# Seven products on three PSUM banks: order and evictions of a Strassen-Winograd pair in an encoder layer

## The chip, the core and the metric

The kernel runs on one core of a Trainium2 chip. The metric is the device time of one execution in microseconds (us); lower is better.

## The reference

One layer of a streaming-encoder trunk on 256 tokens of width 2048, in float32: a SwiGLU feed-forward, a hybrid mixer (chunked mLSTM and stick-breaking attention in parallel branches, merged by gates), a second SwiGLU feed-forward, each with a layer norm behind it, and a gated per-layer embedding at the end.

```python
def _swiglu(x, w1, w3, w2):
    return (jax.nn.silu(x @ w1) * (x @ w3)) @ w2

def reference(x, p, ...):
    x = _layer_norm(ALPHA * x + 0.5 * _swiglu(x, ffn1_w1, ffn1_w3, ffn1_w2), ln1_g, ln1_b)
    mix = _hybrid_mixer(x, w_in, ...)      # x @ w_in: 11 column groups, two branches, two gates
    x = _layer_norm(ALPHA * x + mix, ln2_g, ln2_b)
    x = _layer_norm(ALPHA * x + 0.5 * _swiglu(x, ffn2_w1, ffn2_w3, ffn2_w2), ln3_g, ln3_b)
    x = x + jax.nn.sigmoid(x @ w_ple_gate) * (p @ w_ple_proj)
```

w1 and w3 are 2048 x 5632, w2 is 5632 x 2048.

## The kernel before

**Precision.** Every large matmul is made of three: weights and activations are each split into a rounded high part and the rest, and high x high, high x low and low x high are summed in PSUM. A *weight tile* holds 256 rows by 512 columns, 128 x 2 x 512. `split_one` makes its two parts: ScalarE copies the high part (line 1264), VectorE subtracts for the low one (line 1268). A *unit* is six matmuls (lines 1319 to 1321, twice): one weight tile against 128 tokens.

**Plain groups.** `group` multiplies a block of 512 columns in the plain way: each weight tile serves two units, one for each half of the tokens.

**Pairs.** Of the rest, two blocks of 512 columns are taken together and multiplied by seven products in place of eight (Strassen in Winograd's form). The 2 x 2 blocks are the two halves of the tokens and two halves of the rows on one side, two row halves and two column blocks on the other. `seven` writes the list of units for such a pair: products 1 to 7, each over four *quads* (four steps of 512 rows along the 2048), 28 units, and each of their weight tiles serves a single unit. In the feed-forwards a pair is 512 columns of w1 beside 512 of w3 (`up7`, nine pairs in each of the two), in the mixer two blocks of w_in (`both7`, five pairs). `act` holds the transposed activations, `act.forms` their sums (made by `form_turn`).

**Sums of weights.** Products 5, 6 and 4 use one tile, b11, on which b12, b22 and b21 are added one after the other; product 7 adds b22 onto b12. An addition is either a VectorE instruction (`plus`, line 366) or a DMA issued by GpSimd that adds from HBM (`plus_load`, line 372): in quads of `loaded` products 5 and 7 use the DMA, and all else VectorE. `Weight.loads` lists the raw tiles that must be loaded for a tile, `frees` those that are done with after its split, and `soon` the sums that are issued right behind its split. The sum of product 5 is in `soon` of product 1 of its quad, since it overwrites b11.

**Order and limits.** `seven` returns the units as: product 1 of the first quad; then, quad by quad, product 1 of the next quad and 5, 7, 6, 3; then 4 and 2 of all quads in turn. `in_line` sets one pair behind the other, with the next one's first unit four units before the end. `weave` spreads the pairs' units evenly among the plain groups' (in a feed-forward 252 among 172). Everything is issued in one program order: after each unit, `splits_due` splits weights as long as no more than the second number of `HELD` are in flight, and `loads` issues loads as long as no more raw tiles than the first number are held.

```python
HELD = {"ffn": (11, 6), "mix": (6, 6), "woven": (9, 6), "wide": (11, 6)}
```

A raw tile marked `early` (b12 of a DMA sum) is loaded three places ahead of its turn (`AHEAD`). Work that follows a product is set into the order by `Sched` with delays from `DELAY`.

**PSUM.** Each product has a bank of its own, but 2, which goes on top of 1. As a product ends, `done` is called. In `up7` product 1 is copied out by ScalarE (line 598), 2 goes through Silu on ScalarE, and VectorE adds 6, 7, 5, 4 and 3 to the copies straight from their banks (lines 592 and 630); `both7` is alike (lines 420, 426, 436, 439).

Of the kernel before, what the change touches and what calls it, by code (L numbers as in the profile page):

```python
# [16 lines left out]
D = 2048  # L17
# [6 lines left out]
COL = 512  # L24
# [12 lines left out]

HEAD = 20
# [17 lines left out]
    "alpha": 24.0, "away": 5.0, "sig": 5.0, "form": 18.0, "ln_turn": 3.6, "ln_step": 2.1, "gb": 14.0, "h": 8.0, "silu": 6.0, "late": 9.0, "last": 5.0, "rest": 1.2, "mt": 3.2,  # L56
# [132 lines left out]
def kernel(  # L189
# [159 lines left out]
    def seven(wa, ca, wb, cb, rows, cols, act, done, loaded):  # L349
# [7 lines left out]
        accs = {m: {} for m in range(1, 8)}  # L357
        accs[2] = accs[1]

        def unit(m, i, tile, src, half, sub):  # L360
            return Unit(tile, half, accs[m], src, i, sub, i == 0 and m != 2, i == n - 1,
                        lambda ps, t, m=m: done(m, ps))
# [12 lines left out]
        one, rest, then = [], [], []  # L375
        for i in range(n):
            b11, b12, b22, b21 = (rows_of(w, (4 * i + sub) * P, c, cols)
                                  for w, c, sub in ((wa, ca, 0), (wb, cb, 0), (wb, cb, 2), (wa, ca, 2)))
            m1 = Weight(b11, [b11], [])
            if i in loaded[0]:  # L380
                m5 = Weight(b11, [], [], plus_load(b11, b12.src[0]), m1)
                m5.by_load = True
                m1.soon.append(m5)
            else:
                m5 = Weight(b11, [b12], [], plus(b11, b11, b12), m1)
            if i in loaded[1]:
                assert i in loaded[0]
                m7 = Weight(b12, [b12], [b12], plus_load(b12, b22.src[0]), m1)
                m7.by_load = b12.early = True
                (m6 if i else m1).soon.append(m7)  # L390
            else:
                m7 = Weight(b12, [b12, b22] if i in loaded[0] else [b22], [b12], plus(b12, b12, b22),
                            m1 if i in loaded[0] else m5)
            m6 = Weight(b11, [b22] if i in loaded[1] else [], [], plus(b11, b11, b22), m5)
            m2 = Weight(b21, [], [b21])
            m4 = Weight(b11, [b21], [b11], plus(b11, b11, b21), m6)
            one.append(unit(1, i, m1, act, 0, 0))
            rest.append([unit(5, i, m5, act.forms, 0, 0), unit(7, i, m7, act.forms, 1, 0),
                         unit(6, i, m6, act.forms, 0, 2), unit(3, i, Weight(b22, [], [b22]), act.forms, 1, 2)])
            then += [unit(4, i, m4, act, 1, 2), unit(2, i, m2, act, 0, 2)]  # L400
            then[-1].onto = True
        first = []
        for i in range(n):
            first += one[i + 1:i + 2] + rest[i]
        return one[:1], first, then
# [9 lines left out]
    def both7(w, ca, cb, act, dest, ready, loaded):  # L415

        r, held = {}, {}

        def put(k, t, a, b, op):
            nc.vector.tensor_tensor(out=r[k, t], in0=a, in1=b, op=op)  # L420

        def rest():
            u = r[0, 1]
            put(0, 1, held[7], u, ALU.add)
            z = r[1, 1] = dest(1, 1)
            nc.vector.scalar_tensor_tensor(out=z, in0=u, scalar=-1.0, in1=held[5],
                                           op0=ALU.mult, op1=ALU.subtract)
            ready(1, 1)
# [3 lines left out]
        def done(m, ps):  # L432
            held[m] = ps
            if m == 1:
                r[0, 1] = dest(0, 1)
                nc.scalar.copy(r[0, 1], ps)
            elif m == 2:
                r[0, 0] = dest(0, 0)
                nc.scalar.copy(r[0, 0], ps)
                ready(0, 0)  # L440
            elif m == 6:
                r[1, 0] = dest(1, 0)
                put(0, 1, ps, r[0, 1], ALU.add)
                put(1, 0, held[5], r[0, 1], ALU.add)
                sched.spawn(rest(), DELAY["rest"])
            elif m == 4:
                sched.until(lambda: (1, 1) in r)
                put(0, 1, ps, r[0, 1], ALU.add)
                ready(0, 1)
            elif m == 3:  # L450
                put(1, 0, ps, r[1, 0], ALU.subtract)
                ready(1, 0)
# [112 lines left out]
    def ffn(w1, w3, w2, act, norm, skew=True, ahead=()):  # L565
# [22 lines left out]
        def up7(c):  # L588
            r, held = {}, {}
# [3 lines left out]

            def done(m, ps):
                held[m] = ps
                if m == 1:
                    r["u"] = temp()
                    nc.scalar.copy(r["u"][:], ps)
                elif m == 2:
                    r["g0"] = temp()  # L600
                    activate(r["g0"][:], ps, ACT.Silu)
                    sched.spawn(late(r["u"], r["v"], r["z"], r["g0"]), DELAY["late" if c < n - 1 else "last"])
                elif m == 6:
                    u, v, z = r["u"], temp(), temp()
                    both(u[:], ps, u[:], ALU.add)
                    both(v[:], held[5], u[:], ALU.add)
                    r["v"], r["z"] = v, z
                    sched.spawn(rest(), DELAY["rest"])
                elif m == 4:
                    sched.until(lambda: "rest" in r)  # L610
                    both(r["u"][:], ps, r["u"][:], ALU.add)
                    sched.spawn(silu(r["u"]), DELAY["silu"])
                elif m == 3:
                    both(r["v"][:], ps, r["v"][:], ALU.subtract)

            def rest():
                both(r["u"][:], held[7], r["u"][:], ALU.add)
                both(r["z"][:], held[5], r["u"][:], ALU.add)
# [4 lines left out]
            def silu(x):  # L623
                activate(x[:], x[:], ACT.Silu)
                return
                yield

            def late(u, v, z, g0):
                both(v[:], v[:], g0[:], ALU.mult)
                nc.vector.scalar_tensor_tensor(out=z[:], in0=z[:], scalar=-1.0, in1=u[:], op0=ALU.mult, op1=ALU.mult)  # L630
                drop(2)
                sched.spaced(turn(v, c, 0), DELAY["h"], TURN_GAP)
                sched.spaced(turn(z, c, 1), DELAY["h"] + 2.0, TURN_GAP)
# [3 lines left out]
            return seven(w1, c * COL, w3, c * COL, D, COL, act, done, (range(c == 1, 4), range(c == 1, 4)))  # L637
# [452 lines left out]
    every = (range(4), range(4))  # L1090
# [8 lines left out]
    later = (range(1, 4), range(1, 4))  # L1099
# [114 lines left out]
    splits = {}  # L1214
# [40 lines left out]
    def split_one():  # L1255
# [14 lines left out]
        for f in w.soon:  # L1270
            assert f.raw.tile is not None
            f.make()
            f.made = True
# [83 lines left out]
```

## Time and profile before

| | |
|---|---|
| median of 3 runs | 2169.44 us (2167.12 to 2170.17) |
| the profiled execution: its time | 2169.55 us |
| its span, first to last instruction | 2167.7 us |
| granted TensorE clock | 1.000 |
| TensorE (PE) busy | 2157.4 us |
| VectorE (DVE) busy | 1893.7 us |
| ScalarE (ACT) busy | 1347.1 us |
| GpSimd (POOL) busy | 218.2 us |
| moved by DMA | 535.98 MB |

The page of a profile gives, for one execution, busy times of the engines, a chart in 40 slices, the chain of work that ended last, and groups of instructions: line, engine, operation, tiles and shapes, count, then busy us and mean ns of one, then the idle time just before them and what ended it. "L1264" is line 1264 of the kernel. `raw` are weight tiles as loaded, `split` their parts, `mm` the PSUM banks of units, `ms` those of transposes and other small matmuls, `temp` and `big` tiles in SBUF.

### The profile page before, as it was taken

The page shows a single profiled execution, that of the slowest core. Times are in us where ns is not written, and L with a number is a line of the kernel's source. Part 1 is how long each engine was busy: PE and PEld are TensorE (multiplying, and loading weights), DVE is VectorE, ACT ScalarE, POOL GpSimd, SP SyncE. Part 2 cuts the span into 40 slices and gives each one's busy share as a digit, 9 for nine tenths or more (in the row PEclk, how much of TensorE's full clock was granted, in tenths as well). Part 3 has the DMA queues.
Part 4 walks back from the last instruction along what each step waited for, and adds up shares of the span by engine and source line. Part 5 has one row for each costly group of instructions (what it writes and reads, how often), then busy time and mean ns, then how long its engine had stood idle before and what let it go on. Part 6 is the DMA issues. An engine that isn't in the chain of part 4 may idle for free.

```text
span 2167.7 us, 27662 instructions
## 1 busy us (share of the span) xinstructions
PE 2157.4 (100%) x9798; PEld 1783.9 (82%) x9798; DVE 1893.7 (87%) x2088; ACT 1347.1 (62%) x1658; POOL 218.2 (10%) x186
## 2 busy tenths in 40 slices
PE   9999999999999999999999999999999999999999
PEld 7888888888888888888888888888888888888887
DVE  6899999999998898887878975799999999999974
ACT  7656666656655765677866554556556656656572
POOL 0111111111100000101010000011111111111000
PEclk9999999999999999999999999999999999999999
DMA  9899899999994667978898976679989999999642
GB/s 349 215 275 270 249 270 275 272 280 268 266 318 140 215 218 219 242 218 203 260 272 260 273 260 203 201 192 279 267 245 276 279 266 277 257 276 294 237 166 87
DMA packets 283179, 535.98 MB, mean 247 GB/s; under 512 B 17144, under 2 KB 34464, under 8 KB 283040
## 3 DMA queue, kind: packets, MB, share of 16 engines
q1 hardware_dynamic: 234624, 440.87, 59.9%
q0 software_dynamic: 48416, 93.33, 23.9%
q8 instruction: 77, 1.26, 0.2%
q14 instruction: 62, 0.51, 0.1%
HBM read 527.85 MB, written 6.29 MB: 246 GB/s over the span
## 4 chain that ended last, share of the span: by engine, by line
PE 93%; issue 2%; DMA 2%; DVE 2%; ACT 0%; POOL 0%; SPq 0%; POOLq 0%; DVEq 0%; ACTq 0%
PE mm L1319 30%; PE mm L1321 30%; PE mm L1320 30%; DMA raw<-in_ffn_w_dram 2%; PE ms L293 1%; DVE split L1268 1%; PE ms L519 0%; DVE raw L366 0%; PE ms L984 0%; PE ms L906 0%; PE ms L921 0%; PE ms L997 0%; POOL raw L372 0%; PE ms L1008 0%; DMA actT<-ymaway 0%
## 5 line engine op out<-in xcount | busy, mean ns | idle before, releaser
L1264 ACT CAST split<-raw 128x1024 fp32r<-128x1024 f32 (+1 forms) x1089 | 1089.4, 1044 | 513.8 <-DMA raw<-in_ffn_w_dram 172.7
L1268 DVE TENSOR_TENSOR split<-raw,split 128x1024 fp32r<-128x1024 f32 (+1 forms) x1089 | 1277.8, 1212 | 141.5 <-ACT split L1264 134.6
L1319 PE MATMUL mm<-split,actT 128*128 128x512 f32 x3064 | 1203.0, 393 | 1.2 <-DVE big L420 1.2
L1321 PE MATMUL mm<-split,actT 128*128 128x512 f32 x3064 | 1189.5, 388 | 0.6 <-DVE actT L300 0.6
L1320 PE MATMUL mm<-split,actT 128*128 128x512 f32 x3064 | 1188.4, 388 | 1.0 <-DVE split L1268 1.0
L1321 PEld LDWEIGHTS mm<-split,actT 128*128 128x128 f32 x3064 | 575.8, 188 | 120.7 <-DVE actT L300 1.4
L1320 PEld LDWEIGHTS mm<-split,actT 128*128 128x128 f32 x3064 | 576.6, 188 | 115.9 <-DVE split L1268 3.4
L1319 PEld LDWEIGHTS mm<-split,actT 128*128 128x128 f32 x3064 | 576.3, 188 | 115.5 <-issue 2.6
L372 POOL DMA_DIRECT2D raw<-in_ffn_w_dram x140 | 169.7, 1441 | 1204.9 <-DVE split L1268 809.6
L366 DVE TENSOR_TENSOR raw<-raw 128x1024 f32<-128x1024 f32 x190 | 231.6, 1220 | 1.6
L372 POOL DMA_DIRECT2D raw<-in_w_in_dram x38 | 46.0, 1426 | 505.7 <-DVE split L1268 432.5
L295 ACT CAST actT<-ms 128x512 fp32r<-128x512 f32 x60 | 35.1, 586 | 77.7 <-PE ms L293 73.2
L644 DVE SCALAR_TENSOR_TENSOR big<-mm,big 128x512 f32<-128x512 f32 x112 | 76.5, 685 | 2.9 <-PE mm L1321 2.8
L592 DVE TENSOR_TENSOR temp<-mm,temp 128x512 f32<-128x512 f32 x108 | 73.1, 686 | 1.8 <-PE mm L1321 0.6
L300 DVE TENSOR_TENSOR actT<-ms,actT 128x512 fp32r<-128x512 f32 x60 | 41.1, 687 | 16.5 <-ACT big L299 11.0
L243 ACT ACTIVATE temp<-mm 128x512 f32<-128x512 f32 (+1 forms) x36 | 20.3, 570 | 49.5 <-PE mm L1321 49.5
L239 ACT ACT_TABLE_LOAD x34 | 43.6, 1283 | 0.6
L288 DVE TENSOR_TENSOR actT<-temp,actT 128x512 fp32r<-128x512 f32 x40 | 26.5, 689 | 17.3 <-ACT actT L287 17.2
L1180 DVE TENSOR_TENSOR temp<-temp,big 128x512 f32<-128x512 f32 (+1 forms) x10 | 5.8, 583 | 26.4 <-ACT temp L243 26.4
L287 ACT CAST actT<-temp 128x512 fp32r<-128x512 f32 x40 | 23.9, 620 | 8.0 <-DVE temp L311 7.4
L243 ACT ACTIVATE rstd<-mv,eps 128x1 f32<-128x1 f32 x6 | 1.8, 295 | 41.8 <-DVE mv L502 41.8
L1123 DVE SCALAR_TENSOR_TENSOR big<-big,mm 128x512 f32<-128x512 f32 x8 | 5.5, 686 | 25.3 <-PE mm L1321 25.3
(133 smaller groups left out, 605.6 us busy)
## 6 DMA issues: line engine op xcount, KB each, us to landing
raw<-in_ffn_w_dram SPq DMA_DIRECT2D x527, 512.0 KB, 6.9
raw<-in_w_in_dram SPq DMA_DIRECT2D x144, 512.0 KB, 5.3
raw<-in_ffn_w_dram POOLq DMA_DIRECT2D x140, 512.0 KB, 9.8
raw<-in_w_in_dram POOLq DMA_DIRECT2D x38, 512.0 KB, 9.0
raw<-in_w_out_dram SPq DMA_DIRECT2D x32, 512.0 KB, 5.5
raw<-in_w_ple_gate_dram SPq DMA_DIRECT2D x32, 512.0 KB, 5.2
raw<-in_w_in_dram SPq DMA_DIRECT2D x56, 256.0 KB, 3.8
raw<-in_w_up_m_dram SPq DMA_DIRECT2D x16, 512.0 KB, 6.8
```

What stands on the lines that cost most here:

```text
L239: nc.scalar.preload_act_table_set(table[0])
L295: nc.scalar.copy(dst[:, 0], ps[:])
L300: nc.vector.tensor_tensor(out=dst[:, 1], in0=ps[:], in1=dst[:, 0], op=ALU.subtract)
L366: nc.vector.tensor_tensor(out=out.tile[:, :, :cols], in0=a.tile[:, :, :cols], in1=b.tile[:, :, :cols], op=ALU.add)
L372: nc.gpsimd.dma_start(out=out.tile[:, :, :cols], in_=src, accum_op=ALU.add)
L592: nc.vector.tensor_tensor(out=out, in0=a, in1=b, op=op)
L644: nc.vector.scalar_tensor_tensor(out=xs, in0=ps, scalar=0.5, in1=xs, op0=ALU.mult, op1=ALU.add)
L1264: nc.scalar.copy(hi[:, ks], r[:, ks])
L1268: nc.vector.tensor_tensor(out=lo[:, ks], in0=r[:, ks], in1=hi[:, ks], op=ALU.subtract)
L1319: nc.tensor.matmul(ps, hi, w[0][:, k, :u.cols], start=first, stop=False, skip_group_check=u.onto)
L1320: nc.tensor.matmul(ps, hi, w[1][:, k, :u.cols], start=False, stop=False, skip_group_check=u.onto)
L1321: nc.tensor.matmul(ps, lo, w[0][:, k, :u.cols], start=False, stop=last, skip_group_check=u.onto)
```

## The change

The order of a pair's units is written out (`CHAIN`), and products 1, 6, 7 and 4 accumulate one after the other on one bank, without a new start; ScalarE copies the bank as it stands after each of 1, 6 and 7. Products 5 and 3 do the same on a second bank, and 2 has a third. So the partial sums that VectorE had made are made by the accumulation; signs are turned where the running sums ask for it, one of them in `form_turn`. Quads no longer alternate product by product: product 1 of all quads comes first, with 5 close behind, then 6, 3 and 2, then 7, and 4 at the end. VectorE makes the sum for product 4 right behind the split of product 2 of that quad; the DMA for product 7 is issued behind the splits named in `CHAIN_BEHIND`. Sums asked for whose tile is not loaded yet wait in `asked`. The work after the products is spread: product 2's Silu, then one half of the outputs after product 3 (delay `late0`) and the other after product 4.

```diff
+CHAIN = [(1, 0), (1, 1), (1, 2), (5, 0), (1, 3), (5, 1), (5, 2), (5, 3), (6, 0), (6, 1), (3, 0), (2, 0), (6, 2), (3, 1),
+         (2, 1), (6, 3), (3, 2), (2, 2), (7, 0), (2, 3), (7, 1), (7, 2), (7, 3), (3, 3), (4, 0), (4, 1), (4, 2), (4, 3)]
+CHAIN_BEHIND = (2, 1), (6, 3), (3, 2), (2, 2)
...
-        nc.vector.tensor_tensor(out=s34[:, r], in0=a[0][:, r], in1=s12[:, r], op=ALU.add)
+        nc.vector.scalar_tensor_tensor(out=s34[:, r], in0=a[0][:, r], scalar=-1.0, in1=s12[:, r],
+                                       op0=ALU.mult, op1=ALU.subtract)
...
-        accs = {m: {} for m in range(1, 8)}
-        accs[2] = accs[1]
+        accs = {m: {} for m in (1, 2, 5)}
+        accs[6] = accs[7] = accs[4] = accs[1]
+        accs[3] = accs[5]
...
+            u = Unit(tile, half, accs[m], src, i, sub, i == 0 and m in (1, 2, 5), i == n - 1,
+                     lambda ps, t, m=m: done(m, ps))
...
+        def with_split(w, after):
+            w.by_load = True
+            after.soon.append(w)
...
+            m1 = W[1, i] = Weight(b11, [b11], [])
+            if i in loaded:
                 m5 = Weight(b11, [], [], plus_load(b11, b12.src[0]), m1)
+                with_split(m5, m1)
+                m7 = Weight(b12, [b12], [b12], plus_load(b12, b22.src[0]), m1)
+                b12.early = True
...
+            W[6, i] = Weight(b11, [b22], [], plus(b11, b11, b22), m5)
+            W[3, i] = Weight(b22, [], [b22])
+            W[2, i] = Weight(b21, [b21], [b21])
+            W[4, i] = Weight(b11, [], [b11], plus(b11, b11, b21), W[6, i])
+            with_split(W[4, i], W[2, i])
+        behind = CHAIN_BEHIND
         for i in range(n):
-            first += one[i + 1:i + 2] + rest[i]
-        return one[:1], first, then
+            with_split(W[7, i], W[behind[i]] if i in loaded else W[3, i])
...
+        units = [unit(m, i, W[m, i], *at[m]) for m, i in CHAIN]
+        return units[:1], units[1:], []
...
             def done(m, ps):
                 if m == 1:
+                    keep("g", ps)
+                elif m == 5:
+                    keep("z", ps)
+                elif m == 6:
+                    keep("v", ps)
                 elif m == 2:
+                    both(r["g"][:], ps, r["g"][:], ALU.add)
+                    sched.spawn(silu(r["g"]), DELAY["silu"])
+                elif m == 3:
+                    both(r["v"][:], ps, r["v"][:], ALU.add)
+                    sched.spawn(late(0, r["v"], r["g"]), DELAY["late0"])
+                elif m == 7:
+                    keep("u", ps)
                     sched.spawn(rest(), DELAY["rest"])
                 elif m == 4:
                     sched.until(lambda: "rest" in r)
+                    activate(r["u"][:], ps, ACT.Silu)
+                    sched.spawn(late(1, r["z"], r["u"]), DELAY["late" if c < n - 1 else "last"])
 
             def rest():
+                both(r["z"][:], r["u"][:], r["z"][:], ALU.add)
...
+        asked.extend(w.soon)
+        for f in asked[:]:
+            if f.raw.tile is not None:
+                f.make()
+                f.made = True
+                asked.remove(f)
```

`keep` is a ScalarE copy of the bank into a tile; `both7` changes in the same way, with copies of 1, 5, 6, 7 and 4 and three VectorE operations.

More of the change, by code (lines that the diff above doesn't have):

```diff
@@ L55 @@
 DELAY = {
[L56 removed]
+    "alpha": 24.0, "away": 5.0, "sig": 5.0, "form": 18.0, "ln_turn": 3.6, "ln_step": 2.1, "gb": 14.0, "h": 8.0, "silu": 6.0, "late": 9.0, "late0": 1.0, "last": 5.0, "rest": 1.2, "mt": 3.2,
     "sbt": 4.6, "g0": 3.0, "g1": 4.0, "g2": 12.0, "cv0": 1.0, "cv1": 5.0, "cv2": 1.3,
@@ L356, in seven @@
         n = rows // (4 * P)
-        accs = {m: {} for m in range(1, 8)}
-        accs[2] = accs[1]
+        accs = {m: {} for m in (1, 2, 5)}
+        accs[6] = accs[7] = accs[4] = accs[1]
+        accs[3] = accs[5]
         def unit(m, i, tile, src, half, sub):
-            return Unit(tile, half, accs[m], src, i, sub, i == 0 and m != 2, i == n - 1,
-                        lambda ps, t, m=m: done(m, ps))
+            u = Unit(tile, half, accs[m], src, i, sub, i == 0 and m in (1, 2, 5), i == n - 1,
+                     lambda ps, t, m=m: done(m, ps))
+            u.onto = m not in (1, 2, 5)
+            return u
         def plus(out, a, b):
@@ L373, in plus_load @@
             return make
-        one, rest, then = [], [], []
+        def with_split(w, after):
+            w.by_load = True
+            after.soon.append(w)
+        W = {}
         for i in range(n):
@@ L394, in seven @@
[L394 to L400, printed above, removed]
@@ L415, in both7, with keep, less @@
     def both7(w, ca, cb, act, dest, ready, loaded):
-        r, held = {}, {}
-        def put(k, t, a, b, op):
-            nc.vector.tensor_tensor(out=r[k, t], in0=a, in1=b, op=op)
-        def rest():
[L423 to L428, printed above, removed]
+        r = {}
+        def keep(k, t, ps):
+            if (k, t) not in r:
+                r[k, t] = dest(k, t)
+            nc.scalar.copy(r[k, t], ps)
+        def less(k, t, a):
+            nc.vector.scalar_tensor_tensor(out=r[k, t], in0=a, scalar=-1.0, in1=r[k, t], op0=ALU.mult, op1=ALU.subtract)
+            ready(k, t)
+        def rest():
+            less(1, 1, r[0, 1])
             return
@@ L1088, in ups @@
         return parts[0] + parts[1]
-    every = (range(4), range(4))
+    every = range(4)
     def gate_dest(g):
@@ L1097, in gate_dest @@
         return dest
-    later = (range(1, 4), range(1, 4))
+    later = range(1, 4)
     def pair(g):
```

87 lines of the change are left out of this document (28 added, 59 removed).

## The prediction

> **What bounds the kernel now.** I read the page first, from its busy shares to its chain, then the matmuls in order of time, then busy times by stretch, then the waits. Sections 1, 2 and 4 of the page:
>
> ```profile
> PE 2157.4 (100%) x9798; PEld 1783.9 (82%) x9798; DVE 1893.7 (87%) x2088; ACT 1347.1 (62%) x1658; POOL 218.2 (10%) x186
> PE   9999999999999999999999999999999999999999
> DVE  6899999999998898887878975799999999999974
> PEclk9999999999999999999999999999999999999999
> ...
> PE 93%; issue 2%; DMA 2%; DVE 2%; ACT 0%; POOL 0%; SPq 0%; POOLq 0%; DVEq 0%; ACTq 0%
> ```
>
> TensorE is busy in every slice at the full granted clock, and the chain that ended last is 93% TensorE. A busy matmul is not yet one at its peak, so I look at the distance from start to start. Timeline of PE, the first and last of 24 rows, and the group of one of the three matmul lines:
>
> ```profile
> 399.68 0.39 PE L1320 MATMUL mm<-split,actT 128*128 128x512 f32 x1
> ...
> 404.89 0.39 PE L1319 MATMUL mm<-split,actT 128*128 128x512 f32 x1
> ...
> L1319 PE MATMUL mm<-split,actT 128*128 128x512 f32 x3064 | 1203.0, 393 | 1.2 <-DVE big L420 1.2
> ```
>
> 23 distances in 5.21 us are 0.2265 us each, and 3 x 3064 = 9192 of these matmuls need 2082 us. What is left of the span, 86 us, goes to the 606 small matmuls and to gaps. Span less busy time is 2167.7 - 2157.4 = 10.3 us.
>
> Where is that idle time, and how near are the suppliers? Busy time by stretch (start, tail, first feed-forward, second, mixer):
>
> ```profile
> 0.00:60.00 60.00, 57.41 (x254) 46.73 (x255) 42.18 (x56) 41.50 (x58) 3.55 (x9) 1.00 0.91 320
> ...
> 2050.00:2168.00 118.00, 112.65 (x513) 92.98 (x511) 74.09 (x98) 56.87 (x92) 0.00 (x0) 1.00 0.36 125
> ...
> 150.00:600.00 450.00, 450.00 (x2016) 372.80 (x2015) 425.01 (x419) 279.92 (x297) 67.78 (x56) 1.00 0.95 270
> 1540.00:1950.00 410.00, 409.98 (x1834) 338.98 (x1833) 385.86 (x379) 249.66 (x265) 61.30 (x51) 1.00 0.95 268
> 660.00:1150.00 490.00, 489.64 (x2325) 406.17 (x2325) 404.68 (x541) 338.20 (x507) 36.35 (x30) 1.00 0.76 219
> ```
>
> The columns are PE, PEld, DVE, ACT, POOL, clock, DMA share, GB/s. Start and tail hold 2.6 + 5.0 us of the idle time (the last stretch reaches 0.3 us past the span); 2.7 us lie between them, and that is all that a change which leaves the matmuls as they are can plainly win. In the feed-forwards VectorE is at 94% and the DMA engines at 0.95. TensorE never waits, yet both are close behind it. The mixer has room: 83% and 0.76.
>
> **The change, part by part.** *Matmuls.* Each pair has 28 units of six matmuls before and after; fewer banks and start flags take none away. Cost 0.
>
> *Evictions.* The split of a weight tile, and the rows of what goes and what comes:
>
> ```profile
> L1264 ACT CAST split<-raw 128x1024 fp32r<-128x1024 f32 (+1 forms) x1089 | 1089.4, 1044 | 513.8 <-DMA raw<-in_ffn_w_dram 172.7
> L1268 DVE TENSOR_TENSOR split<-raw,split 128x1024 fp32r<-128x1024 f32 (+1 forms) x1089 | 1277.8, 1212 | 141.5 <-ACT split L1264 134.6
> L366 DVE TENSOR_TENSOR raw<-raw 128x1024 f32<-128x1024 f32 x190 | 231.6, 1220 | 1.6
> L592 DVE TENSOR_TENSOR temp<-mm,temp 128x512 f32<-128x512 f32 x108 | 73.1, 686 | 1.8 <-PE mm L1321 0.6
> L420 DVE TENSOR_TENSOR big<-mm,big 128x512 f32<-128x512 f32 x25 | 17.2, 687 | 2.3 <-PE mm L1321 2.0
> L598 ACT COPY temp<-mm 128x512 f32<-128x512 f32 x18 | 10.6, 586 | 9.8 <-PE mm L1321 9.7
> ```
>
> A feed-forward pair (`up7`) now has 8 VectorE operations on products, and 5 after; a mixer pair (`both7`) 6, and 3 after. Over 18 + 5 pairs that is 69 x 0.686 = 47 us less of VectorE. ScalarE gets 3 more copies a pair: 69 x 0.586 = 40 us more. VectorE in a feed-forward falls from 94% to 91%, ScalarE rises from 62% to 65%. Neither engine is on the path, so this is worth at most what TensorE still idles between start and tail: I take 1 us of gain, bounds 0 and 2.7. The weight sums stay 190 on VectorE and 178 on GpSimd; the sign change in `form_turn` costs nothing.
>
> *New wait: the bank.* Products 6, 7 and 4 may start only when ScalarE has copied product 1, 6, 7; product 3 waits for the copy of 5. By the new order and the weave (252 product units among 172 others) 5 or 6 units lie between 1 and 6, and 4 in the other three places: 4 x 6 x 0.2265 = 5.4 us of cover. Queued behind a waiting matmul is everything on TensorE. What L598's copy of product 1 waited for (time and times of 18), and the longest standstills of ScalarE at a split (waits; total, times, longest):
>
> ```profile
>   PE mm L1321: 9.7, 12
> ...
> ACT split L1264 <- DMA raw<-in_ffn_w_dram: 172.7, 90, 4.1
> ACT split L1264 <- DVE raw L366: 160.8, 82, 5.0
> ACT split L1264 <- PE mm L1320: 73.5, 64, 4.2
> ```
>
> In 12 of 18 cases ScalarE stood ready before TensorE had ended, so the copy mostly comes at once. Even 5.0 + 0.59 us passes the cover by only 0.2 us. Cost 0; the upper bound, 1 us at each of 23 pairs, is a rival.
>
> *Moved: sums made by a DMA.* This is the step that I charge. Product 5's weights come from an accumulating DMA that GpSimd may issue only once the split of product 1's weights of that quad is done, since it overwrites them. How long it takes (GpSimd's and ScalarE's timeline, then landings of all 178 and of two that met few loads):
>
> ```profile
> 321.74 2.42 POOL L372 DMA_DIRECT2D raw<-in_ffn_w_dram  x2 [7.27 <-DVE split L1268]
> 386.67 2.42 POOL L372 DMA_DIRECT2D raw<-in_ffn_w_dram  x2 [7.24 <-DVE split L1268]
> 330.79 1.06 ACT L1264 CAST split<-raw 128x1024 fp32r<-128x1024 f32 x1 [0.63 <-DMA raw<-in_ffn_w_dram]
> 334.79 4.89 ACT L1264 CAST split<-raw 128x1024 fp32r<-128x1024 f32 x5 [2.94 <-DMA raw<-in_ffn_w_dram]
> DMA to landing us min/median/max: 5.7/9.7/14.0
> ...
> DMA to landing us min/median/max: 6.0/7.1/8.2
> ```
>
> The first of two issued at 321.74 releases ScalarE 9 us later, the second 13 us later. The two GpSimd rows are the same quad of two pairs: a pair lasts 64.9 us and has 28 product weights and about 9.5 others, 1.73 us each.
>
> How much time is there? A split can start when the weight six places before it has left TensorE (the waits for PE above: this limit is reached). Five weights are then still ahead, 6.8 us where all are product weights of one unit; less ScalarE's 1.04 and VectorE's 1.21 us the lead is 4.5 us. With u units from product 1 to product 5 of a quad the DMA may take 4.5 + 1.36u - 0.3 - 2.3 us before TensorE stands. In the old order u is 9 or 10: 14.1 us or more, so even the slowest (14.0) fits. In the new order u is 6, 7 and 5 for quads 1, 2, 3: 10.1, 11.4 and 8.7 us. Quad 1 (9 us, first of two) fits. Quad 2 is issued 1.4 us behind it and lands like a second one, 13 us after the first: 11.6 against 11.4. Quad 3 has 8.7 us for a DMA with median 9.7: 1.0 us short in each of 18 pairs, 18 us; at the quickest 5.7 us nothing, at 14.0 us 95 us. In the old order these come by twos among a steady flow of loads; in the new one few loads are asked for in that stretch, so I choose nearer to the second landing line than to the median: 0.5 us a pair, +9 us.
>
> [...]
>
> *Moved: loads.* At most 11 raw tiles are held in this stretch. In the new order product 1's tiles of all four quads are held from the start to product 4 (4 tiles), and all four of product 7 are loaded before the first is used (4 more). With quad 3's second row block little is left: counting through the lists, the tiles for product 2 of quads 2 and 3 are asked for 2 to 5 weights before their split, and the plain weights there 2 to 7, where the old order has 9 to 14 for both. Two weights (2 units) leave 4.5 + 2.7 - 2.3 = 4.9 us, some more where SP finds a page free earlier. The landings of all loads, and the median of the feed-forward's:
>
> ```profile
> DMA to landing us min/median/max: 2.6/5.9/15.3
> ...
> raw<-in_ffn_w_dram SPq DMA_DIRECT2D x527, 512.0 KB, 6.9
> ```
>
> The median is 2.0 us too long, the quickest fits, the slowest is 10 us too long; with four accumulating DMAs of product 7 in the same stretch long ones are likely, while SP's earlier issue helps. I take 0.3 us a pair: +5 us, bounds 0 and 18 x 2 = 36. The order of product 7's DMAs on GpSimd, moved past three to five weights, costs nothing while they wait for their own load alone. In the mixer I charge nothing: five pairs, with VectorE and DMA far from full; bounds 0 and 5.
>
> *Sum.* The profiled execution took 2169.55 us, 1.9 around its span, and the median of the runs is 2169.44. -1 + 0 + 9 + 5 = +13: **2182.4 us**.
>
> **The rivals.** *Hidden after all, 2169.4 (2166 to 2173).* If the DMAs of product 5 take about 7 us once loads pause, as in the second landing line, all three fit and the lead of 4.5 us swallows the late loads. For it speaks that the old order has leads just as short without any standstill; against it, that DMA share 0.95 leaves little to catch up with. [...]
>
> *Faster, 2164.4.* VectorE's 47 us and the early sums of product 4 (half of the 190 sums, whose wait on ScalarE's side is 160.8 us) remove the 2.7 us between start and tail, and as much again that the modelled ends of the matmuls may hide: 5 us. It decides only where no new standstill arises at all.
>
> *The bank chain, 2192.4.* ScalarE, held by a late DMA at a split, reaches the copy of product 7 late, and product 4 stands 1 us in each of 23 pairs: +23 us. Against it speak the 12 of 18 above.
>
> **How the numbers follow.** Forecast (late weights) 0.48, hidden 0.35, bank chain 0.10, faster 0.07. 0.2% is 4.3 us, about what a measurement of this kernel can tell from no change. Slower by more is 0.48 + 0.10 = 0.58, within 0.35, faster 0.07. The range reaches from 2165.5 (the hidden case) to 2205, where a quad 3 that is 1.0 us short and loads 1.0 us late in every pair (18 + 18) would lie; what is beyond has about 0.15. The forecast's own range is 2174 to 2205.
>
> **What would show it.** Right: busy VectorE near 1847 us and ScalarE near 1387; TensorE losing some 13 us in feed-forward stretches, with ScalarE's split waiting for a DMA for more than 172.7 us in total. The step on product 5 is wrong if its DMAs land within 8.7 us; the step on loads, if TensorE stands nowhere near product 2. The whole is wrong if matmuls start closer than 0.2265 us apart, or if TensorE waits for a ScalarE copy.

## The result and the profile after

| | before | after |
|---|---|---|
| median (runs) | 2168.34 us (4) | 2207.89 us (4; 2200.45 to 2215.39) |
| profiled execution: time, span | 2169.55, 2167.7 us | 2215.39, 2213.3 us |
| granted TensorE clock | 1.000 | 0.997 |

The changed kernel is slower by 39.5 us, ratio 1.0181 [1.0168, 1.0195]. The forecast said slower, 2182.4, and the range ended at 2205.0, so the sign was right and the size was not. The profiled execution of after is the longest of its four; its span is 45.6 us above that of before, and shares are read from it with that in mind.

The page of after, engines, chart and chain:

```profile
PE 2175.4 (98%) x9798; PEld 1783.0 (81%) x9798; DVE 1845.6 (83%) x2019; ACT 1373.3 (62%) x1724; POOL 215.8 (10%) x186
...
DVE  6998898898988798777777876798898888898974
...
PEclk9999999999999999999999999999999999999999
...
PE 7%; DMA 1%; DVE 0%; issue 0%; ACT 0%; POOL 0%; SPq 0%; ACTq 0%; POOLq 0%
```

VectorE is 48 us less busy and ScalarE 26 us more. The count of matmuls is the same. TensorE idles 37.9 us (span less busy) in place of 10.3, and its busy time is 18 us longer. The shares of this chain add up to 8%: it is followed back only a little way from the end and says nothing about the rest. So I go by stretch, with the columns of before (start, tail, first feed-forward, second, mixer):

```profile
0.00:60.00 60.00, 57.38 (x257) 46.59 (x258) 41.73 (x55) 42.27 (x59) 2.99 (x9) 1.00 0.89 315
2095.00:2213.50 118.50, 113.31 (x516) 93.46 (x514) 74.52 (x98) 56.87 (x92) 0.00 (x0) 1.00 0.36 125
...
150.00:600.00 450.00, 440.02 (x1943) 357.61 (x1942) 397.72 (x386) 277.20 (x306) 63.48 (x53) 1.00 0.94 265
1540.00:1950.00 410.00, 400.32 (x1765) 325.51 (x1764) 359.27 (x347) 251.69 (x278) 57.74 (x49) 1.00 0.92 260
660.00:1150.00 490.00, 486.72 (x2302) 403.87 (x2301) 401.98 (x538) 339.06 (x514) 33.94 (x28) 0.99 0.74 219
```

Start and tail lose what they lost before. The feed-forwards, where TensorE had no gap at all, now lose 10.0 and 9.7 us, about 1.5 us for each pair of 65 us; the mixer loses 2.9 us more. VectorE falls by 27 us in each feed-forward stretch, in part because less of the work fits into it (1943 matmul records in place of 2016). What the engines stand for (waits: time, times, longest) and the groups behind them:

```profile
ACT split L1271 <- DMA raw<-in_ffn_w_dram: 234.5, 105, 6.9
DVE split L1275 <- ACT split L1271: 231.6, 170, 5.2
ACT split L1271 <- DVE raw L374: 74.0, 34, 4.2
PE mm L1329 <- DVE split L1275: 14.4, 24, 1.2
PE mm L1328 <- ACT temp L601: 9.4, 4, 2.9
...
L374 DVE TENSOR_TENSOR raw<-raw 128x1024 f32<-128x1024 f32 x190 | 231.1, 1218 | 0.0
L601 ACT COPY temp<-mm 128x512 f32<-128x512 f32 x72 | 41.7, 579 | 17.9 <-PE mm L1330 17.8
```

ScalarE's split now waits 234.5 us for DMAs of feed-forward weights (172.7 before), VectorE 231.6 us for ScalarE (134.6). The wait for VectorE's sums falls from 160.8 to 74.0, so that part of the relief is real. TensorE waits 24 times for a late low part and four times for a copy of its bank (`L601` is `keep`).

The row of 234.5 us holds two kinds of DMA: plain loads, issued by SyncE (line 1238 before, 1245 after), and accumulating DMAs, issued by GpSimd (372, 380). Who waited for each over the whole run (us, times), plain loads first, before, then after:

```profile
  ACT split L1264: 9.2, 9
  ACT split L1264: 172.5, 89
...
  ACT split L1271: 118.7, 56
  ACT split L1271: 154.7, 73
```

So before, ScalarE waited almost only for accumulating DMAs, and these waits fall a little. What is new is the wait for plain loads: 118.7 us from 9.2. Put down to products in the feed-forwards, it is 59 us at plain weights and 29 at product 2's last two quads. The waits for accumulating DMAs change place: product 5's quads 1 to 3 rise from 21 to 107 us, product 7 falls from 112 to 23.

How such a copy comes to be late is seen in one place of a pair, ScalarE, then TensorE, then GpSimd:

```profile
293.86 2.95 ACT L1271 CAST split<-raw 128x1024 fp32r<-128x1024 f32 x3 [0.31 <-ACT split L1271]
303.75 1.04 ACT L1271 CAST split<-raw 128x1024 fp32r<-128x1024 f32 x1 [6.94 <-DMA raw<-in_ffn_w_dram]
304.70 0.58 ACT L601 COPY temp<-mm 128x512 f32<-128x512 f32 x1
...
302.94 0.39 PE L1330 MATMUL mm<-split,actT 128*128 128x512 f32 x1
305.33 0.50 PE L1328 MATMUL mm<-split,actT 128*128 128x512 f32 x1 [2.00 <-ACT temp L601]
...
290.88 1.20 POOL L380 DMA_DIRECT2D raw<-in_ffn_w_dram  x1 [11.65 <-PE mm L1329]
292.29 1.19 POOL L380 DMA_DIRECT2D raw<-in_ffn_w_dram  x1 [0.21 <-issue]
300.32 1.20 POOL L380 DMA_DIRECT2D raw<-in_ffn_w_dram  x1 [6.84 <-DVE raw L374]
```

A plain weight's load is late, ScalarE stands 6.94 us in front of its split, and the copy of product 6 is queued behind that split. Product 7 may not start until the copy is done. GpSimd issues the accumulating DMAs of product 7 in the same microseconds. By the lists (the order in which loads and splits are issued) this weight is asked for three weights ahead of its split; I call that its *notice*. Of some 180 tiles counted in the first feed-forward, 16 have a notice of at most 3 in the changed kernel, none before.

To see where TensorE loses time I took, for each matmul, its distance from the one before less 0.227 us, and put it down to the unit by the order in which units are issued (us, after the first 36 us of the span; one profile each):

| standstill before | before | after | 13 raw tiles | product 7 without DMAs | (5, 3) later | own bank for 7 |
|---|---|---|---|---|---|---|
| plain units | 9.6 | 27.7 | 14.3 | 13.8 | 18.8 | 26.8 |
| product 5, last quad | 0.1 | 5.3 | 4.2 | 0.9 | 0.7 | 3.8 |
| product 7, first quad | 0.2 | 12.4 | 0.6 | 0.6 | 5.5 | 1.2 |
| product 2, last quad | 0.0 | 4.5 | 1.0 | 0.2 | 4.6 | 12.8 |
| all | 18.4 | 62.0 | 29.8 | 22.7 | 42.9 | 58.9 |

43.6 us of the 45.6 are in it. The largest rows are plain units and product 7's first unit. Of the plain units' 27.7, about 12 lie in the feed-forwards (1 before), nearly half of it right behind the first unit of product 7 and the last of product 2, and about 11 in the mixer's pairs (4 before). By the same mapping I read the *lead*, from the end of VectorE's split to the first matmul that uses it, as the median of the 18 feed-forward pairs. At product 5's last quad it falls from 5.4 us to 1.3, with 8 of the 18 below 0 (a first matmul needs the high part alone). From product 6's first quad to product 7's second it is 0.4 to 1.7, where before has 2.3 to 4.7; it is 2.0 at product 7's last and above 3 at product 4. The leads named in the expectations below come from an earlier count and differ by some tenths; the -0.1 at product 5's last quad is not borne out by this one.

### The profile page after: what moved, and what is told of

Same layout as the page of the kernel before. It is cut to its first block, busy times and chain, and to the rows that moved or that the text cites. A ratio compares the mean times of both kernels' runs of the same rounds, so it can differ in the third digit from the quotient of the medians.

```text
span 2213.3 us, 27560 instructions
## 1 busy us (share of the span) xinstructions
PE 2175.4 (98%) x9798; PEld 1783.0 (81%) x9798; DVE 1845.6 (83%) x2019; ACT 1373.3 (62%) x1724; POOL 215.8 (10%) x186
## 5 line engine op out<-in xcount | busy, mean ns | idle before, releaser
L1275 DVE TENSOR_TENSOR split<-raw,split 128x1024 fp32r<-128x1024 f32 (+1 forms) x1089 | 1280.7, 1210 | 241.3 <-ACT split L1271 231.6
L1271 ACT CAST split<-raw 128x1024 fp32r<-128x1024 f32 (+1 forms) x1089 | 1087.4, 1043 | 537.3 <-DMA raw<-in_ffn_w_dram 234.5
L601 ACT COPY temp<-mm 128x512 f32<-128x512 f32 x72 | 41.7, 579 | 17.9 <-PE mm L1330 17.8
L247 ACT ACTIVATE temp<-ms,gbT 128x128 f32<-128x128 f32 x64 | 24.1, 460 | 5.5 <-PE ms L524 5.5
```

The lines of the kernel that those rows point to most:

```text
L247: nc.scalar.activation(out, in_, func, **kw)
L601: nc.scalar.copy(r[k][:], ps)
L1271: nc.scalar.copy(hi[:, ks], r[:, ks])
L1275: nc.vector.tensor_tensor(out=lo[:, ks], in0=r[:, ks], in1=hi[:, ks], op=ALU.subtract)
```

## The experiments

Four theories were set against each other. **A, late loads**: too few raw tiles and too short notice in the stretch of products 2 and 7, with ScalarE held at a split. **B, the bank**: the waits of 6, 7 and 4 for copies are themselves the price. **C, product 5**: its accumulating DMAs come too late. **D, VectorE**: the sums for 6 and 4 bunch and fill it. Below, "excess" is the median less that of before in the same batch; that of the change is +39.5 us, and the intervals are some 2 to 5 us wide on either side.

**Thirteen raw tiles in place of eleven.**

```diff
-HELD = {"ffn": (11, 6), ...
+HELD = {"ffn": (13, 6), ...
```

> The changed kernel with room for 13 raw weight tiles in the feed-forwards in place of 11. Theory A (late loads: product 1's four tiles and product 7's four take the 11 places, so tiles near product 7 are asked for too late, ScalarE stands at their split, and the copy of product 6 is queued behind it): more than half of the 39.5 us goes, 2170 to 2188 us; ScalarE's waits at a split for a DMA of the feed-forward weights fall from 234.5 us to under 175, and TensorE's stalls before product 7 quad 0 (12.4 us) to under 4. Theory B (the bank chain by itself: ScalarE's copies are too slow for the units between): nothing moves, 2200 to 2212 us. Theory C (the accumulating DMAs of product 5 come too late, the prediction's larger term): nothing moves, since they depend on product 1's split and not on the room.

Measured 2182.28 us, 1.0068 [1.0051, 1.0085], excess +13.9. Two tiles take away 26 us. Waits of this kernel:

```profile
ACT split L1271 <- DMA raw<-in_ffn_w_dram: 109.1, 54, 5.0
PE mm L1329 <- DVE split L1275: 5.3, 12, 0.7
```

The wait for DMAs is less than half, its longest 5.0 us; by issuer, that for plain loads falls from 118.7 to 34.0 us, that for accumulating DMAs from 154.7 to 114.0. By the lists no notice is shorter than 5. TensorE's waits for a copy on `L601` are gone although the banks are as they were. This bears out A.

**The change's order on banks of its own, with the old evictions.**

```diff
-        accs = {m: {} for m in (1, 2, 5)}
-        accs[6] = accs[7] = accs[4] = accs[1]
-        accs[3] = accs[5]
+        accs = {m: {} for m in range(1, 8)}
+        accs[2] = accs[1]
... done(), rest() and late() as before the change
```

> The changed kernel's order of units and sums, but each product on a bank of its own and the evictions of the kernel before (VectorE adds from the banks; only 2 goes on top of 1). Theory A: the splits are as late as before, so TensorE still waits for them, but no longer for a copy: 10 to 17 us of the 39.5 go (the four waits of 2 to 3 us before product 7, and what the lower clock costs behind them), 2190 to 2200 us. Theory B: back to the kernel before, 2166 to 2175 us. Theory C: unchanged or slower by VectorE's extra work, 2203 to 2215 us.

Measured 2217.01 us, 1.0226 [1.0201, 1.025], excess +48.7: 9 us worse than the change. The order alone, without any shared bank, is as dear, so B falls as the main cause. It lies above all three numbers, nearest to C's case with VectorE's extra work; that A's number was missed because that work came back is only argued.

**The old order with eight raw tiles.**

```diff
-HELD = {"ffn": (11, 6), ...
+HELD = {"ffn": (8, 6), ...
```

> The kernel before with room for 8 raw weight tiles in the feed-forwards in place of 11, nothing else. Theory A: short notice for loads costs time in the old order too, without any bank chain: 2180 to 2215 us, ScalarE's waits for feed-forward DMAs above 234 us in all. Theories B and C: the old order has no chain and asks for product 5's sums early enough, so 2166 to 2174 us.

Measured 2166.99 us, 0.9994 [0.9985, 1.0003]. No change, against A's number. By the lists the shortest notice is then 3 weights, and 38 of 180 tiles have at most 5, more than in the changed kernel (27). But only 1 of them has at most 3, where the changed kernel has 16. So a notice of 4 or 5 costs nothing in the old order, where product 7's DMAs come one quad at a time; whether 2 or 3 alone would cost anything there, this run does not show.

**Product 5's last quad later, and product 2 before 3.**

```diff
-CHAIN = [... (5, 2), (5, 3), (6, 0), (6, 1), (3, 0), (2, 0), (6, 2), ...
+CHAIN = [... (5, 2), (6, 0), (5, 3), (6, 1), (2, 0), (3, 0), (6, 2), ...
```

> The changed kernel with product 5 of quad 3 one place later (behind product 6 of quad 0) and product 2 of quad 0 ahead of product 3 of quad 0, so that the last accumulating DMA of product 5 has one more unit. Theory C: most of the 39.5 us goes, 2172 to 2188 us. Theory A: only the stalls at product 5 quad 3 go, 5.3 us in the profiled execution, 2198 to 2207 us. Theory B: unchanged, or slower by a few us since product 6 now follows product 1 one unit sooner.

Measured 2192.11 us, 1.0111 [1.0092, 1.0129], excess +23.8: 16 us less than the change, more than A allowed and less than C.

**Without the sums for product 4** (92 VectorE operations).

```diff
-            W[4, i] = Weight(b11, [], [b11], plus(b11, b11, b21), W[6, i])
-            with_split(W[4, i], W[2, i])
+            W[4, i] = Weight(b11, [], [b11])
```

> The changed kernel without the 92 VectorE sums for product 4 (b21 is not added, so product 4's values are not the reference's). Theory D (VectorE is full between product 6 quad 0 and product 7 quad 0, 22.9 of 23 us in one pair, because the sums for 6 and those for 4 are made there together; the lead lost at product 5 can't be won back): 2170 to 2188 us, the median lead at product 7 quad 0 back above 2.5 us from 1.1. Theory A (late loads alone): loads are as late as before, 2197 to 2212 us. Theory C (product 5's DMAs alone): the stalls at product 5 stay, what follows them does not, 2190 to 2200 us.

Measured 2199.52 us, 1.0149 [1.0134, 1.0164], excess +32.0: 7 us less, inside A's numbers and at the upper end of C's, outside D's. The lead at product 7's first unit is then 3.7 us in place of 1.3, yet TensorE stands 16.9 us there; 11.7 us of its waits are for a copy. D is a small part.

**Product 2 spread through product 7's stretch, product 3 ended ahead of it**, eleven tiles.

```diff
-... (6, 1), (3, 0), (2, 0), (6, 2), (3, 1), (2, 1), (6, 3), (3, 2), (2, 2), (7, 0), (2, 3), (7, 1), (7, 2), (7, 3), (3, 3), ...
-CHAIN_BEHIND = (2, 1), (6, 3), (3, 2), (2, 2)
+... (6, 1), (3, 0), (6, 2), (3, 1), (6, 3), (3, 2), (3, 3), (7, 0), (2, 0), (7, 1), (2, 1), (7, 2), (7, 3), (2, 2), (2, 3), ...
+CHAIN_BEHIND = (3, 1), (6, 3), (3, 2), (3, 3)
...
                 elif m == 2:
+                    sched.spawn(late(0, r["v"], r["g"]), DELAY["silu"] + 3.5)
                 elif m == 3:
-                    sched.spawn(late(0, r["v"], r["g"]), DELAY["late0"])
```

> The changed kernel with the same work in another order: product 2, and with it the sums for product 4, spread through the stretch of product 7 (order 1 1 1 5 1 5 5 5, 6 6 3 6 3 6 3 3, 7 2 7 2 7 7 2 2, 4 4 4 4; product 3 ends before 7). Theory D: the sums no longer meet those of product 6, 2172 to 2190 us. Theory A: product 3 gives its tiles back before 7, the loads of b21 come with more notice but for the last two, 2180 to 2195 us. Theory C: unchanged, 2200 to 2212 us.

Measured 2169.32 us, 1.0004 [0.9995, 1.0014], excess +1.8. That is below all the numbers given. The order alone takes away nearly all of it, with the same banks, copies, tiles and DMAs (half of the outputs move with product 2). No notice is shorter than 4, and the lead at product 7's first unit is 3.9 us. Since the sums for product 4 move along with the loads, the run doesn't tell A from D. Product 7's DMAs are still asked for behind four product units in a row, and the median landing of a feed-forward's loads is 7.6 us, as in the change.

**Thirteen tiles and the swaps together** (the two diffs above).

> The changed kernel with both earlier edits, 13 raw tiles in the feed-forwards and product 5 quad 3 one place later. If the two causes add, 26 and 16 us of 39.5, nothing is left: 2166 to 2172 us. If both only top up the same lead (theory D, VectorE stays full behind product 5), they overlap: 2173 to 2182 us.

Measured 2169.71 us, 1.0009 [0.9999, 1.0018], excess +2.2: 26 and 16 us add up.

**All three** (spread order, thirteen tiles, (5, 3) behind (6, 0)).

> Spread product 2, 13 raw tiles and product 5 quad 3 one place later, on the three banks. Theories A, C and D together: TensorE's matmuls are the bound again, 2164 to 2171 us. If more than 2175 us, a cause is still missing (the bank chain, theory B, would be the next).

Measured 2165.48 us, 0.9991 [0.9982, 1.0001], excess -2.0.

**Product 7 without its accumulating DMAs** in the quads that use one.

```diff
-                m7 = Weight(b12, [b12], [b12], plus_load(b12, b22.src[0]), m1)
+                m7 = Weight(b12, [b12], [b12])
...
-            with_split(W[7, i], W[behind[i]] if i in loaded else W[3, i])
+            if i not in loaded:
+                with_split(W[7, i], W[3, i])
```

> The changed kernel without the accumulating DMAs of product 7 in the quads that use them (b22 is not added to b12, so product 7's values are not the reference's). The late loads of plain tiles and of product 2's tiles share the DMA engines with just these four. If the loads are late because the room is full and these DMAs make each one longer: 2180 to 2195 us, ScalarE's longest wait for a feed-forward DMA under 5 us from 6.9. If the short notice is enough by itself: 2197 to 2208 us. If only product 5's DMAs count: 2200 to 2212 us.

Measured 2171.57 us, 1.0018 [1.0009, 1.0027], excess +3.7: 36 us less, better than any number given, with eleven tiles and the change's order. Landings of a feed-forward's loads (SPq) and accumulating DMAs (POOLq), KB each, median us; of after, then of this kernel with its wait (its line numbers are one higher):

```profile
raw<-in_ffn_w_dram SPq DMA_DIRECT2D x527, 512.0 KB, 7.6
raw<-in_ffn_w_dram POOLq DMA_DIRECT2D x140, 512.0 KB, 8.9
```

```profile
raw<-in_ffn_w_dram SPq DMA_DIRECT2D x527, 512.0 KB, 5.4
raw<-in_ffn_w_dram POOLq DMA_DIRECT2D x70, 512.0 KB, 8.1
...
ACT split L1272 <- DMA raw<-in_ffn_w_dram: 113.6, 63, 5.2
```

The same 527 loads land in 5.4 us in place of 7.6. Of the 16 tiles with a notice of at most 3, the 8 whose landing can be told took a median of 9.3 us in the change and take 4.8 here. ScalarE's wait for plain loads is 21.0 us from 118.7. Notices are as short as in the change, and so is the lead (0.4 us at product 6's last quad, 0.7 in the change). So short notice and a short lead cost little once the loads are quick, and in this order product 7's DMAs make them slow. That it is their bunching isn't shown: the run also leaves out half of the accumulating DMAs (47 of 536 MB) and the waits of product 7's own weights, and the spread order paid almost nothing with all of them there, asked for just as close together.

**The order of "all three" on banks of its own, with the old evictions.**

> The best order so far (product 2 spread, 13 raw tiles, product 5 quad 3 one place later), but a bank for each product and the evictions of the kernel before. If the three banks and ScalarE's copies give nothing once the order is right: 2164 to 2168 us as with them (2165.48). If the chain of copies costs there: lower, 2160 to 2164 us. If VectorE's 69 fewer operations are what the order needs: 2170 to 2185 us.

Measured 2172.15 us, 1.0016 [1.0007, 1.0025], excess +4.3. In a good order the shared banks are worth 6.6 us (2172.15 less 2165.56, the next run of the same batch). The time lies in the last of the ranges given, that of VectorE's 69 operations; but the run brings back old banks, copies and operations together and does not tell them apart.

**"All three" in five rounds.**

> Product 2 spread, 13 raw tiles, product 5 quad 3 one place later, three banks, once more against the kernel before in more rounds: 2164 to 2167 us, ratio 0.999, if the few idle microseconds between the matmuls that the kernel before has are won; ratio 1.000 if the first difference was chance.

Measured 2165.56 us, 0.9989 [0.998, 0.9998], excess -2.3. It is faster than both kernels, by a tenth of a per cent against before; the interval only just leaves out 1, and that of the first run of this kernel holds 1. Its waits and stretches:

```profile
ACT split L1271 <- DMA raw<-in_ffn_w_dram: 54.9, 38, 3.5
...
150.00:600.00 450.00, 450.00 (x2015) 372.57 (x2014) 413.11 (x397) 294.17 (x317) 66.21 (x55) 1.00 0.98 272
1540.00:1950.00 410.00, 410.00 (x1837) 339.48 (x1836) 374.82 (x360) 267.25 (x289) 61.38 (x51) 1.00 0.97 269
```

TensorE has no gap in the feed-forwards again, with VectorE at 92% where it was at 94%.

**Product 5's last quad without its DMA.**

```diff
-                m5 = Weight(b11, [], [], plus_load(b11, b12.src[0]), m1)
-                with_split(m5, m1)
+                m5 = Weight(b11, [], [], plus_load(b11, b12.src[0]) if i < 3 else None, m1)
+                if i < 3:
+                    with_split(m5, m1)
```

> The changed kernel without the accumulating DMA for product 5 of quad 3 (its values are not the reference's). Theory C: the wait for this one DMA is gone, so at least as much as moving it one place won, 2180 to 2193 us, and the lead at product 5 quad 3 is above 2 us from -0.1. If it was the order of products 2 and 3 of quad 0 in that experiment that helped: 2200 to 2212 us.

Measured 2201.11 us, 1.0152 [1.0135, 1.017], excess +33.2: the DMA itself is worth 6 us, less than C asked for. That left open why the swaps gained 16.

**Each swap alone.** (5, 3) behind (6, 0):

> Only (5,3) and (6,0) change places; product 2 stays where the change put it. The earlier run with both swaps gained 16 us, and the run without the DMA of (5,3) only 7. If what is gained at product 5 is the late DMA alone, some 7 us: about 2201. Rival: the unit that moves between gives VectorE's lead time to recover before product 6, which the run without the DMA did not change, and this swap holds all 16: about 2192.

Measured 2193.47 us, 1.0113 [1.0098, 1.0128], excess +26.2, 13 us less than the change. (2, 0) ahead of (3, 0):

> Only (2,0) and (3,0) change places: one weight of product 2 is loaded and freed one unit earlier. If the raw tiles' room sets the price, an earlier release of one tile is worth what is left of the 16 us, some 9: about 2199. Rival: nothing, 2205 to 2210, and the swap at product 5 holds all.

Measured 2207.93 us, 1.0188 [1.0173, 1.0203], excess +40.6: nothing. The swap at product 5 holds the gain, as the rival expectations said. It is worth 7 us more than leaving the DMA out. In its profile the lead is 2.3 us at product 2's second quad (1.0 in the change, 1.8 without the DMA) and 2.6 at product 7's first (1.3 and 2.1); whether that difference is the rest is only argued.

**A bank of its own for products 7 and 4**, all else as in the change.

```diff
-        accs = {m: {} for m in (1, 2, 5)}
-        accs[6] = accs[7] = accs[4] = accs[1]
+        accs = {m: {} for m in (1, 2, 5, 7)}
+        accs[6] = accs[1]
+        accs[4] = accs[7]
...
-            u = Unit(tile, half, accs[m], src, i, sub, i == 0 and m in (1, 2, 5), i == n - 1,
+            u = Unit(tile, half, accs[m], src, i, sub, i == 0 and m in (1, 2, 5, 7), i == n - 1,
```

> Products 7 and 4 start a bank of their own; copies, sums and order stay as in the change. The sums of 1 and 6 are thereby left out of the output. It takes away just the wait of product 7 for the copy of product 6. If that wait adds to a late load what would else be swallowed: the 12 us of standstills at product 7's first unit and the halved clock beside them go, 2190 to 2196. Rival: the late weights of the same stretch are late whatever the bank does, and TensorE stands a few units on: 2203 to 2208, with product 2's last quad and product 7's second in the place of product 7's first.

Measured 2209.88 us, 1.0188 [1.0171, 1.0205], excess +42.6: nothing gained, 2 us above the rival's range. TensorE's first and second matmul line of this kernel (line numbers are one higher than in the change):

```profile
L1329 PE MATMUL mm<-split,actT 128*128 128x512 f32 x3064 | 1204.0, 393 | 5.3 <-ACT split L1272 5.2
L1330 PE MATMUL mm<-split,actT 128*128 128x512 f32 x3064 | 1194.7, 390 | 18.6 <-DVE split L1276 17.5
```

No matmul of a pair waits for a copy any more. The 12.4 us at product 7's first unit became 1.2, and product 2's last quad, the pair's next unit, went from 4.5 to 12.8. The late weights stop TensorE at the pair's next unit anyway. The waits for a copy, among the longest single ones of TensorE in the profile of the change, were not a cause.

## Why the prediction was right or wrong

*Direction and mechanism.* Right. Nothing was to be won where TensorE had no gap, and the order moved loads and DMAs to where they come late. ScalarE's wait for DMAs rose above 172.7 us as foretold, to 234.5, though that sign was a poor one: the row is mostly accumulating DMAs, and the plain loads in it went from next to nothing to over a third. TensorE stands near product 2. Matmuls do not start closer together than before (0.226 us apart from 299.77 to 302.94 us of after).

*VectorE and ScalarE.* Busy 1845.6 against 1847 foretold, and 1373.3 against 1387. Of ScalarE's miss 3.8 us are three table loads fewer (1.283 us each), which I had not seen, and 2.0 the splits; the rest I did not trace. The gain was put at 1 us; the two comparisons of shared with own banks give 9 us in the change's order and 6.6 in the good one. That is lead won, not idle time of before, so the bound of 2.7 us was a bound on the wrong thing for the second order: with own banks that order is at +4.3.

*Product 5's last quad, +9.* The size was nearly right, in part by luck: moving the unit is worth 13 us, the DMA itself 6. In one pair GpSimd issues it at 264.94 and ScalarE's split that waits for it starts 8.7 us later, just what I had allowed:

```profile
264.94 1.20 POOL L380 DMA_DIRECT2D raw<-in_ffn_w_dram  x1 [3.23 <-DVE split L1275]
...
273.67 1.06 ACT L1271 CAST split<-raw 128x1024 fp32r<-128x1024 f32 x1 [1.29 <-DMA raw<-in_ffn_w_dram]
```

In the 14 pairs whose split waits for it, it lands after a median of 7.5 us, and within 8.7 in 11 of them. So by the prediction's own sign the reason given, one DMA that is 1.0 us too slow, is wrong in most pairs, and the choice near the second landing line held; the stretch of that line had few loads in flight but a DMA share of 1.04 (150 to 159 us of before). ScalarE waits for product 5's quads 1, 2 and 3 alike, 35 to 37 us each, and the lead wears down over all three. What I left out is that the lead is spent there and not won back before product 4, so that later units have little left for a late load. The 4.5 us of lead stood in the sum for product 5 and again, unspent, in the sum for loads.

*Late loads, +5.* **This is the step that failed.** I took 0.3 us a pair between bounds of 0 and 36 us in total. Two more tiles, an edit that touches the loads alone, gave back 26 us, and ScalarE's wait for plain loads went with it, from 118.7 to 34.0 us; removing product 7's DMAs gave back 36 us and the spread order 38, though these two change more than the loads. So the term was some 26 of the 39.5 us, or more, where I had 5; with product 5's swap on top of thirteen tiles only 2 us are left. Three readings went wrong. The prediction named the four DMAs of product 7 in that stretch and then let "SP's earlier issue" offset them, with no row for that. The landing median of before (6.9 us) was used for a stretch with four accumulating DMAs in it; the median over all loads of the feed-forwards is 7.6 in after, and 5.4 without product 7's DMAs, and the tiles with the shortest notice took 9.3. And the full lead was assumed, as said above.

*The bank, 0.* Right in price, although the cover was too thin: it was set against ScalarE's longest standstill before, 5.0 us, and after has 6.94. The prediction called itself wrong as a whole if TensorE waited for a copy. It did, four times, and the run with a bank of its own for 7 shows that this cost nothing by itself. That test was badly chosen: a wait that is seen isn't yet a cost.

*The mixer, 0.* It lost 2.9 us of busy time in the stretch read, within the bounds of 0 and 5. Counted by distances between matmuls as in the table, from its first pair to its last, it lost 6 (13.7 us from 7.5), slow matmuls at the halved clock included (0.42 us apart in place of 0.227), which is just above them.

*The rivals.* "Hidden" took some 7 us for product 5's DMAs once loads pause; in the 14 pairs above the median was 7.5 us, but the late loads were not swallowed. Whether accumulations get quicker when loads pause, no run here tells apart. What was measured is the other side: without product 7's DMAs the feed-forwards' loads landed in a median of 5.4 us in place of 7.6, with 47 of 536 MB left out.

## What to carry to other kernels

Costs that sit close together in the order draw on one lead: take the lead off once, where it is first spent, and let the next step start from what is left. Where a reordering puts transfers of another queue among loads with short notice, count the notice of each tile and price the loads by how long they take in that crowded stretch, not by the median of a kernel that has no such stretch; then thin out the transfers or spread the short-notice tiles, either of which took away nearly all here, or hold more tiles, which took away two thirds. Before a wait for a DMA is called a late load, split it by the queue that issued it. To see whether the wait that a trace names is the cause, remove just that wait: here the standstill moved one unit on and the time stayed.

## What the runs showed of the hardware

The granted clock halved after some standstills of TensorE inside the run, which before shows only after its last matmul (clock 0.50 from 2167.39 us on). TensorE at three ends of a standstill in after, and the stretches behind two of them:

```profile
442.73 0.50 PE L1328 MATMUL mm<-split,actT 128*128 128x512 f32 x1 [2.87 <-ACT temp L601]
...
1074.22 0.80 PE L1328 MATMUL mm<-split,actT 128*128 128x512 f32 x1 [3.28 <-ACT temp L721]
...
1834.37 0.79 PE L1328 MATMUL mm<-split,actT 128*128 128x512 f32 x1 [2.56 <-ACT temp L601]
```

```profile
1073.50:1080.00 6.50, 5.78 (x15) 4.51 (x16) 5.21 (x6) 5.82 (x12) 0.00 (x0) 0.50 1.07 338
443.00:447.00 4.00, 4.00 (x19) 3.27 (x19) 3.79 (x5) 3.48 (x4) 0.00 (x0) 1.00 1.09 273
```

After 3.28 and 2.56 us the next matmul takes 0.80 and 0.79 us at clock 0.50; after 2.87 us it takes 0.50 at clock 1.00. So the length of the standstill alone doesn't decide; what else does, these runs do not show. Clock records of after show half clock for 6.8, 3.4 and 3.4 us within the run, from 1073.21, 1175.61 and 1834.38 us on, which adds up to 13.6 us at half speed, some 6.8 us lost at most.
